# A rotary-embedding kernel: first slab whole, two rows of slab 5 loaded early, slab 7 loaded by GpSimd

**Chip, cores, metric.** One Trainium2 chip, one of its cores. The metric is the device time of one execution in microseconds (us). The span in a profile is 1.8 us shorter than the time (160.4 against 162.2).

## The reference

`x` is 16 x 512 x 1024 float32. Each row of 1024 is 16 heads of 64, and each head is rotated by tables that depend on the position:

```python
x1, x2 = x[..., :half_dim], x[..., half_dim:]
rotated = np.concatenate([x1 * cos - x2 * sin,
                          x1 * sin + x2 * cos], axis=-1)
```

33.55 MB are read and 33.55 MB written, with little arithmetic between.

## The kernel before

The input is cut into 8 slabs of 4 MB: 128 partitions, in each 8 rows of 1024 float32 (32 KB, contiguous in HBM). Five slabs have a place on the chip. ScalarE casts a slab to bfloat16, VectorE does three instructions on it, ScalarE casts it back into the slab's own place, and the store goes out from there. SyncE issues the loads, ScalarE the stores. Load 5 needs the place of slab 0, so it waits until store 0 has landed; load 6 waits for store 1, load 7 for store 2.

```python
nb = 2; slots = 5
nslabs = batch // nb              # 8
rpp = nb * seq // P               # 8 rows per partition
W = rpp * dim                     # 8192 elements = 32 KB

def load(s):
    slab[s] = slabs.tile([P, W], f32, tag="slab", name="slab")
    return nc.sync.dma_start(out=slab[s], in_=dram(x, s))

load(0)
# ... tables cos, sin by nc.gpsimd.dma_start; then load(1) .. load(4) ...

def cast(u):
    s, r, n = u
    if r == 0:
        xb[s] = xpool.tile([P, W], bf16, tag="xb", name="xb")
    nc.scalar.copy(out=view(xb[s], r * dim, (1, n * dim)),
                   in_=view(slab[s], r * dim, (1, n * dim)))

passes = []                       # (slab, first row, rows)
for s in range(nslabs):
    n = rpp if 1 <= s < nslabs - 2 else rpp // 2
    passes += [(s, r, n) for r in range(0, rpp, n)]

cast(passes[0])
for i, (s, r, n) in enumerate(passes):
    if i + 1 < len(passes):
        cast(passes[i + 1])       # the cast of the next pass stands first
    # ... VectorE: tensor_mul, tensor_mul, tensor_add ...
    nc.scalar.copy(out=xs, in_=xu)
    if r + n == rpp:
        nc.scalar.dma_start(out=dram(out_flat, s), in_=slab[s])
        if s + slots < nslabs:
            load(s + slots)
```

Slabs 0, 6 and 7 go in two half passes each (called 6a, 6b, 7a, 7b below), the others whole.

## Time and profile before

| | before |
|---|---|
| time, median of 6 runs | 162.13 us (162.07 to 162.65) |
| span of the profiled run | 160.4 us |
| bytes moved, mean rate | 67.24 MB, 419 GB/s |
| busy: VectorE, ScalarE | 68%, 71% |
| slab 0 landed, slab 1 landed | 13.3, 23.0 us |
| load 5, load 6, load 7 landed | 85.2, 104.6, 123.9 us |
| store 0 issued, store 7 (the last) issued | 37.1, 145.3 us |

The bytes at the rate of the loads that run alone (16 slabs of 9.72 us, 155.5 us) make up nearly the whole span of 160.4, so the DMA engines are the bound here and neither compute engine, busy 68% and 71%, is. A landing is read from the timeline wherever an engine stood idle for it: the cast of slab 5 starts at 85.22, and its bracket says that the DMA released it. The quoted lines are in the prediction. Two words for what follows: a packet is the unit in which the trace records what a DMA engine moves, and a completion is one of the 16 packets of 4 bytes that the trace has for every transfer besides its rows (128 on each of q1 and q10 for 8 slabs, before).

### The profile page before, as it was taken

To read this page: it belongs to the slowest core of one execution; us is meant where nothing else is said; L and a number is where in the kernel's file an instruction comes from. 1 tells how busy PE (TensorE), PEld (TensorE's weight loads), DVE (VectorE), ACT (ScalarE), POOL (GpSimd) and SP (SyncE) were. 2 spreads that over 40 slices of the span, in tenths; PEclk is the share of its full clock that TensorE was granted. 3 is DMA by queue.
4 is the path that set the end of the run, shared out by engine and by line. 5 is a ranking of instruction groups with operands and counts; after the bars stand their busy time and mean duration, and the time that the engine had idled before them with its cause. 6 is when DMAs were issued, how large, how long until landed. Compare 5 with 4: busy or idle time off the path is not lost.

```text
span 160.4 us, 169 instructions
## 1 busy us (share of the span) xinstructions
PE 1.0 (1%) x8; PEld 0.8 (1%) x8; DVE 108.5 (68%) x34; ACT 113.5 (71%) x23; POOL 3.4 (2%) x12
## 2 busy tenths in 40 slices
PE   0011000000000000000000000000000000000000
PEld 0010000000000000000000000000000000000000
DVE  0003799999989979997996099939749599930000
ACT  3006939998998999899907997099995999462000
POOL 7000000000000000000000000000000000000000
DMA  7999999999999999999999999999999999999995
GB/s 245 425 409 409 474 425 400 466 441 392 384 400 400 507 400 400 466 441 392 441 474 392 433 482 392 425 482 400 400 507 400 400 474 433 392 449 466 392 433 221
DMA packets 2368, 67.24 MB, mean 419 GB/s; under 512 B 288, under 2 KB 288, under 8 KB 320
## 3 DMA queue, kind: packets, MB, share of 16 engines
q1 hardware_dynamic: 1152, 33.55, 49.5%
q10 hardware_dynamic: 1152, 33.55, 48.4%
q0 software_dynamic: 64, 0.13, 0.2%
HBM read 33.69 MB, written 33.55 MB: 419 GB/s over the span
## 4 chain that ended last, share of the span: by engine, by line
DMA 59%; ACT 17%; issue 9%; DVE 4%; SPq 0%; ACTq 0%; POOLq 0%
DMA slab<-in_x_dram 39%; DMA out_dram<-slab 15%; ACT slab L146 11%; ACT xb L119 6%; DMA raw<-in_cos_dram 4%; DVE xb L140 1%; DVE xb L143 1%; DVE slab L140 1%; SPq L62 0%; ACTq L146 0%; POOLq L167 0%
## 5 line engine op out<-in xcount | busy, mean ns | idle before, releaser
L119 ACT CAST xb<-slab 128x4096 bf16<-128x4096 f32 (+1 forms) x11 | 56.6, 5155 | 27.5 <-DMA slab<-in_x_dram 26.2
L146 ACT CAST slab<-xb 128x4096 f32<-128x4096 bf16 (+1 forms) x11 | 56.6, 5153 | 3.5 <-DVE xb L143 3.5
L140 DVE TENSOR_TENSOR slab<-xb,tab 128x4096 bf16<-128x4096 bf16 (+1 forms) x11 | 35.9, 3260 | 19.9 <-ACT xb L119 19.8
L140 DVE TENSOR_TENSOR xb<-xb,tab 128x4096 bf16<-128x4096 bf16 (+1 forms) x11 | 35.9, 3261 | 0.3
L143 DVE TENSOR_TENSOR xb<-xb,slab 128x4096 bf16<-128x4096 bf16 (+1 forms) x11 | 35.9, 3261 | 0.3
L110 DVE CAST tab<-acc 128x1024 bf16<-128x1024 f32 x1 | 1.2, 1225 | 12.5 <-PE acc L104 12.5
L119 ACT ACT_TABLE_LOAD x1 | 1.3, 1283 | 0.7 <-PEq L167 0.7
L104 PE MATMUL acc<-tab,pick 128*128 128x128 bf16 x8 | 1.0, 305 | 11.5 <-POOL tab L98 11.5
L92 POOL TENSOR_SCALAR_AFFINE_SELECT pick<-pick 128x128 bf16<-128x128 bf16 x4 | 1.0, 288 | 0.1
L104 PEld LDWEIGHTS <-pick 128*128 128x128 bf16 x8 | 0.8, 136 | 11.4 <-issue 8.0
L73 POOL DMA_DIRECT2D raw<-in_cos_dram x1 | 0.7, 674 | 0.8 <-POOLq L167 0.8
L89 POOL MEMSET pick<- 128x512 bf16 x1 | 0.5, 543 | 0.0
L98 POOL CAST tab<-raw 128x256 bf16<-128x256 f32 x1 | 0.4, 396 | 6.9 <-DMA raw<-in_sin_dram 6.9
L73 POOL DMA_DIRECT2D raw<-in_sin_dram x1 | 0.5, 534 | 0.0
L167 POOL MEMSET const-float32-0.0<- 128x1 f32 x1 | 0.1, 99 | 0.2 <-issue 0.2
L167 POOL MEMSET const-bfloat16-1.0<- 128x1 bf16 x1 | 0.1, 102 | 0.0
L167 POOL MEMSET const-uint8-127<- 128x1 uint8 x1 | 0.1, 102 | 0.0
L167 POOL MEMSET const-float32-1.0<- 128x1 f32 x1 | 0.1, 99 | 0.0
## 6 DMA issues: line engine op xcount, KB each, us to landing
slab<-in_x_dram SPq DMA_DIRECT2D x8, 4096.0 KB, 24.5
out_dram<-slab ACTq DMA_DIRECT2D x8, 4096.0 KB, 26.6
raw<-in_cos_dram POOLq DMA_DIRECT2D x1, 64.0 KB, 7.0
raw<-in_sin_dram POOLq DMA_DIRECT2D x1, 64.0 KB, 9.0
```

What stands on the lines that cost most here:

```text
L73: table[i] = nc.gpsimd.dma_start(out=view(raw, i * TR * half, (1, TR * half)), in_=bass.AP(tensor=src.tensor, offset=src.offset, ap=[[TR * ...
L89: nc.gpsimd.memset(pick, 0.0)
L92: nc.gpsimd.affine_select(out=part, in_=part, compare_op=mybir.AluOpType.not_equal, fill=1.0 if g < G else -1.0, base=-(g % G), pattern=[[ ...
L98: nc.gpsimd.tensor_copy(out=tab1, in_=raw)
L104: nc.tensor.matmul(view(acc, (i * rpp + g * TR) * hd + h * half, (hd, TR), (1, half)), view(pick, (i * h * G + g) * P, (1, P)), view(tab1, ...
L110: nc.vector.tensor_copy(out=tab, in_=acc)
L119: nc.scalar.copy(out=view(xb[s], r * dim, (1, n * dim)), in_=view(slab[s], r * dim, (1, n * dim)))
L140: nc.vector.tensor_mul(out=t, in0=xu, in1=view(tab, a + r * hd, (hd, n), (0, nh), (1, hd)))
L143: nc.vector.tensor_add(out=xu, in0=xu, in1=view(t2, half, (hd, n * nh), (-half, 2), (1, half)))
L146: nc.scalar.copy(out=xs, in_=xu)
L167: nc = _bacc.Bacc("TRN2", target_bir_lowering=False, num_devices=1)
```

## The change

Its intent, as far as the code tells: let slab 0 go through in fewer instructions; have 1 MB of slab 5 on the chip before any place is free, in a buffer of its own; and give load 7 a queue where it need not stand behind load 6.

```diff
+    E = 2 * dim
+    ahead = singles.tile([P, E], f32, tag="ahead")
     def load(s):
+        queue = nc.sync if s < nslabs - 1 else nc.gpsimd
+        a = E if s == slots else 0
         slab[s] = slabs.tile([P, W], f32, tag="slab", name="slab")
-        return nc.sync.dma_start(out=slab[s], in_=dram(x, s))
+        return queue.dma_start(out=view(slab[s], a, (1, W - a)),
+                               in_=dram(x, s, a, W - a))
@@ after the loads 1 to 4
+    nc.sync.dma_start(out=ahead, in_=dram(x, slots, 0, E))
@@ cast
-        nc.scalar.copy(out=view(xb[s], r * dim, (1, n * dim)),
-                       in_=view(slab[s], r * dim, (1, n * dim)))
+        a = E if s == slots else 0
+        nc.scalar.copy(out=view(xb[s], r * dim + a, (1, n * dim - a)),
+                       in_=view(slab[s], r * dim + a, (1, n * dim - a)))
+        if a:
+            nc.scalar.copy(out=view(xb[s], 0, (1, a)), in_=ahead)
@@ passes
-        n = rpp if 1 <= s < nslabs - 2 else rpp // 2
+        n = rpp if s < nslabs - 2 else rpp // 2
```

## The prediction

> **What bounds the kernel now.** I read first the slices and queues of the page, then the chain that ended last, then the timeline.
>
> ```profile
> DMA  7999999999999999999999999999999999999995
> ...
> DMA packets 2368, 67.24 MB, mean 419 GB/s; under 512 B 288, under 2 KB 288, under 8 KB 320
> ...
> q1 hardware_dynamic: 1152, 33.55, 49.5%
> q10 hardware_dynamic: 1152, 33.55, 48.4%
> ```
>
> The DMA engines are full in every slice but the first and the last. Each queue has 1152 packets for 8 transfers, 144 each: 128 rows of 32 KB and 16 completions. So on each of 16 engines a slab is 8 packets of one row and one completion.
>
> ```profile
> 13.33 7.11 ACT L119 CAST xb<-slab 128x4096 bf16<-128x4096 f32 x2 [11.31 <-DMA slab<-in_x_dram]
> ...
> 23.05 7.02 ACT L119 CAST xb<-slab 128x8192 bf16<-128x8192 f32 x1 [2.61 <-DMA slab<-in_x_dram]
> ...
> 85.22 7.02 ACT L119 CAST xb<-slab 128x8192 bf16<-128x8192 f32 x1 [5.05 <-DMA slab<-in_x_dram]
> ...
> 145.28 0.34 ACTq L148 DMA_DIRECT2D out_dram<-slab  x1
> ```
>
> Slab 0 lands at 13.33 and slab 1 at 23.05: one slab alone costs 9.72 us, or 1.215 us per row and engine. Fifteen more slabs (7 loads, 8 stores) give 13.3 + 15 x 9.72 = 159.1, against a span of 160.4. Compute has slack: at most 7.02 + 7.01 us of ScalarE per slab against 19.4 us of transfer. The last store is issued at 145.28 but can't start moving before store 6 is through; counted back from the end, 160.4 - 0.9 - 9.7 = 149.8. So the compute tail has about 4 us of slack[...].
>
> ```profile
> 37.11 24.39 DMA out_dram<-slab
> ...
> 61.59 23.61 DMA slab<-in_x_dram
> ...
> 99.00 24.93 DMA slab<-in_x_dram
> ```
>
> This is the chain: store 0 frees slab 0's place, load 5 follows; load 7 follows store 2. Each takes 24 us, not 9.7, since loads and stores take turns on the engines: 2 x 9.72 = 19.4, and 4 to 5 us of queue.
>
> ```profile
> raw<-in_cos_dram POOLq DMA_DIRECT2D x1, 64.0 KB, 7.0
> raw<-in_sin_dram POOLq DMA_DIRECT2D x1, 64.0 KB, 9.0
> ```
>
> These two lines matter most for the change. A table has 4 KB per engine, 0.15 us of work. Issued at 1.24 and 1.91, they land at 8.25 and 10.9, 2.7 us apart: two turns (4 KB of data, then a completion), each behind a 32 KB row of load 0 (2 x 1.215, and the small ones). **The engines take turns by packets, not by bytes**; a small packet pays for a whole turn.
>
> [...]
>
> **The change, part by part.**
>
> *Whole first slab.* Two half passes become one. VectorE keeps its time (6 x 2.29 = 13.7 against 3 x 4.43 = 13.3). Store 0 comes later: 13.33 + 7.02 + 13.3 + 7.01 = 40.7 instead of 37.1. Loads fill the 3.6 us, since five are queued. Alone it costs nothing: the bytes are the same and the DMA never idles.
>
> *Two rows of slab 5 early.* It moves 1 MB, so no bytes are saved. The cast becomes two, of 6144 and 2048 elements: by the size, 5.3 + 1.9 us for 7.0, so 0.2 us more. But "ahead" is 128 rows of 8 KB: 8 packets of 8 KB per engine and one completion, so 9 turns. It sits behind load 4 on SyncE's queue, when stores are already running:
> - Load 3 ends at 32.8 + 9.7 = 42.5. Store 0 starts moving at about 44.5 (3.8 us after its issue). Load 4 has had 2 us alone; its other 7.7 us take 15.4 us: done at 60. Store 0 is done at 62 and lands at about 63.
> - Ahead: 9 turns beside a 1.215 us store row, and 8 x 0.30 us of its own: 13.3 us where bytes alone ask for 2.4. It ends at 73.5. Store 1 gets 8 rows in that time and lands at about 76.
> - The rest of slab 5 (24 KB rows) waits behind ahead though its place was free at 63. Eight turns of 0.91 + 1.215 and one completion: 17 to 18 us, landing at 91 (before 85.2). Store 2 runs beside it and lands at about 93 (before about 99).
>
> So the early rows make slab 5 late and the stores early, and the stores drain ahead of the compute.
>
> *Load 7 on GpSimd's queue.* On SyncE's queue it waited behind load 6. Now it is issued when store 2 lands, at 93, while load 6 has only begun (at 91). From about 96 three queues take turns. Load 6 has about 6 of 8 rows left: 6 x 3 x 1.215 = 21.9, so it lands at about 118 (before 104.6). Load 7 lands at 122 to 123, no better than 123.9 before.
>
> *What that does to the end.* ScalarE works in order: the first cast of slab 6 stands before the last cast of slab 5, and so before store 5. From load 6 at 117.6:
> - cast 6a 3.6, cast-out of slab 5 7.0, issue and cast 6b 4.0: 132.2
> - VectorE on 6b, 7a and 7b, 6.95 each with small waits on casts 7a and 7b: 154.0
> - cast-out of 7b 3.6: store 7 issued at 157.6 (before 145.3)
> - store 7 alone: 9.7 and 2.7 of issue and landing: 170.3; span about 171.
>
> The DMA would idle about 10 us after store 5. The time is 1.8 above the span (162.2 against 160.4), so this sum gives 172.8.
>
> **The rivals.**
> *A: nothing happens (span 160 to 161).* Needed: turns go by bytes for 8 KB rows, or several rows of a SyncE transfer share a packet, so that ahead takes about 5 us. Then load 5 lands at 85, load 6 at 105, load 7 at 123, and the DMA stays full to the end: 162.2. For it: the DMA line of nines, equal bytes, and that the order of transfers is worth nothing while both queues have work; also that someone wrote these parts to fit a tuned kernel. Against it: the two table loads. But those were GpSimd's, with 512 B rows in one 4 KB packet; how 8 KB rows from SyncE are packed, nothing here shows.
> *B: ahead does hurt, but less.* Delays of a few us in GpSimd's issue let load 6 finish sooner; phases of a turn count for 1 us each. Load 6 at 110 to 114 gives a span of 164 to 168, time 166 to 170. If load 7 then is the last to matter (after it 3.6 + 6.95 x 2 + 3.6 + waits = 21.4, as between 123.9 and 145.3 before), a landing after 126.5 costs us for us.
> *C: worse.* If GpSimd's rows are cut into 4 KB packets, load 7 gets a ninth of each round, lands near 140 and ends the kernel: 140 + 21.4 + 12.4 + 0.9 = 175 span.
> *D: faster.* [...] Over 2% can't come out of this unless the start changes, which no part touches.
>
> **Range and chances.** The main sum (172.8) with B around it has about 0.6, A about 0.35. Lags I can't fix by a few us move the main sum mostly down, so I say 169.5, range 161.5 to 174.5, which holds A as well. Faster 0.03, same 0.36, slower 0.61.
>
> **What would show each step.** Ahead: its issue to landing, or the gap from the landing of slab 4 (cast 4 is not its witness, ScalarE is busy) to the cast of slab 5; the cast of 6144 should start near 91, not 85, released by the DMA. Turns: the rows of ahead under 16 KB in the packet line, and store 1 landing near 76. Load 7: GpSimd's issue at about 93, the cast of slab 6 released near 118. End: DMA slices below 9 after slice 33, last store issued near 157. If the cast of slab 5 comes at 85 and the DMA line stays at 9 up to the end, the step "a small row pays a whole turn" is wrong, and the time will be 162. If load 6 lands before 108 although ahead was slow, the three-way sharing is wrong.

## More of the kernel before

In the trace before, the record of load 1's landing (23.03) follows the end of its last completion (22.58) by 0.45 us. The views of the profile don't list single packets and landings; where the text speaks of the trace's records, they were read from the stored trace.

## The result, and the profile after

Six runs of the changed kernel took 165.89, 166.53, 169.28, 170.25, 171.76 and 171.97 us: median 169.76, against 162.13 before. By the rule that a run over 1.5% above the fastest of its kernel counts as slow, the first two are fast and the other four slow; the clock was 1.0 in all. The ratio of the fast runs is 1.0246 (95% interval 1.0212 to 1.028): slower. Ratios here are the mean time of one kernel's fast runs over that of the other's of the same rounds, so not quite the ratio of the medians. The kernel before stayed within 0.6 us in these rounds, so the spread belongs to the changed kernel; run e8 below looks at it.

The profile is of the fastest run (span 164.1). First its slices and queues, from the page:

```profile
DMA  7999999899989999999999998998989989891885
...
q10 hardware_dynamic: 1152, 33.55, 47.4%
q1 hardware_dynamic: 1152, 29.36, 42.4%
q0 software_dynamic: 208, 4.33, 6.1%
```

The DMA line is nearly full (8 or 9) from slice 2 to slice 36 of 40; the 1 after it is 4 us in which hardly anything moved. SyncE's queue (q1) moves 4 MB less but has as many packets as before: the early rows came as 128 packets of 8 KB and 16 completions. Here a row is a packet, of 8, 24 or 32 KB.

Two lines of the table by stretches, before and after (stretch and its length; busy time of PE, weight loads, VectorE, ScalarE and GpSimd; clock, DMA share, GB/s). Before:

```profile
124.00:157.50 33.50, 0.00 (x0) 0.00 (x0) 15.35 (x7) 17.79 (x5) 0.00 (x0) 1.00 0.99 427
```

After:

```profile
124.00:157.50 33.50, 0.00 (x0) 0.00 (x0) 20.63 (x9) 24.50 (x7) 0.00 (x0) 1.00 0.87 376
```

Here the time goes: in the last stretch the compute engines have more left to do and the DMA waits for them. The timeline after tells why:

```profile
89.02 5.31 ACT L129 CAST xb<-slab 128x6144 bf16<-128x6144 f32 x1 [5.11 <-DMA slab<-in_x_dram]
...
94.40 0.56 POOL L69 DMA_DIRECT2D slab<-in_x_dram  x1 [83.02 <-ACT xb L129]
...
113.23 3.60 ACT L129 CAST xb<-slab 128x4096 bf16<-128x4096 f32 x1 [10.18 <-DMA slab<-in_x_dram]
...
152.13 0.34 ACTq L159 DMA_DIRECT2D out_dram<-slab  x1
```

(The bracket of load 7's issue names a cast, but the issue follows the landing of store 2, at 93.85, by 0.55 us, as it does within 0.01 us in e1, e3, e4, e6, e8 and e12 below, so store 2 is what it waited for.) Slab 5 comes at 89.0 (before 85.2), load 7 is issued at 94.4 (before 99.0), slab 6 comes at 113.2 (before 104.6), and the last store is issued at 152.1 (before 145.3). And the issues with their time to landing:

```profile
slab<-in_x_dram POOLq DMA_DIRECT2D x1, 4096.0 KB, 28.5
slab<-in_x_dram SPq DMA_DIRECT2D x1, 3072.0 KB, 26.0
ahead<-in_x_dram SPq DMA_DIRECT2D x1, 1024.0 KB, 62.0
```

The early rows, issued at 10.05, land at 72.05. Load 4, just ahead of them in the queue, lands at 59.9 by the trace's record of landings; so 1 MB took 12.1 us. The rest of slab 5, issued at 63.0, spends 26 us on 3 MB. In the chain of waits the end now hangs on load 6:

```profile
55.24 21.01 DMA out_dram<-slab
...
76.30 36.90 DMA slab<-in_x_dram
...
113.23 3.60 ACT xb L129
116.83 6.92 ACT slab L157
...
148.50 3.60 ACT slab L157
```

Store 1 lands at 76.25, load 6 follows and takes 36.9 us (the chain before held load 7 there, with 24.9 us), and after it there is compute to the end.

### The profile page after: what moved, and what is told of

It reads as the page before. It is cut to its first block, busy times and chain, and to the rows that moved or that the text cites. A ratio compares the mean times of both kernels' runs of the same rounds, so it can differ in the third digit from the quotient of the medians.

```text
span 164.1 us, 166 instructions
## 1 busy us (share of the span) xinstructions
PE 1.0 (1%) x8; PEld 0.8 (1%) x8; DVE 108.3 (66%) x31; ACT 113.5 (69%) x22; POOL 3.9 (2%) x13
## 3 DMA queue, kind: packets, MB, share of 16 engines
q10 hardware_dynamic: 1152, 33.55, 47.4%
q1 hardware_dynamic: 1152, 29.36, 42.4%
q0 software_dynamic: 208, 4.33, 6.1%
## 4 chain that ended last, share of the span: by engine, by line
DMA 43%; ACT 35%; DVE 12%; issue 2%; ACTq 0%; SPq 0%
DMA slab<-in_x_dram 30%; ACT slab L157 19%; ACT xb L129 15%; DMA out_dram<-slab 13%; DVE xb L151 4%; DVE xb L154 4%; DVE slab L151 4%; ACTq L159 0%; ACTq L157 0%; SPq L69 0%
## 5 line engine op out<-in xcount | busy, mean ns | idle before, releaser
L129 ACT CAST xb<-slab 128x8192 bf16<-128x8192 f32 (+2 forms) x10 | 54.8, 5481 | 30.5 <-DMA slab<-in_x_dram 29.3
L157 ACT CAST slab<-xb 128x8192 f32<-128x8192 bf16 (+1 forms) x10 | 56.5, 5650 | 7.4 <-DVE xb L154 7.3
L151 DVE TENSOR_TENSOR slab<-xb,tab 128x8192 bf16<-128x8192 bf16 (+1 forms) x10 | 35.7, 3571 | 27.0 <-ACT xb L129 21.1
L154 DVE TENSOR_TENSOR xb<-xb,slab 128x8192 bf16<-128x8192 bf16 (+1 forms) x10 | 35.7, 3572 | 0.3
L151 DVE TENSOR_TENSOR xb<-xb,tab 128x8192 bf16<-128x8192 bf16 (+1 forms) x10 | 35.7, 3572 | 0.3
L69 POOL DMA_DIRECT2D slab<-in_x_dram x1 | 0.6, 557 | 83.0 <-ACT xb L129 83.0
L132 ACT CAST xb<-ahead 128x2048 bf16<-128x2048 f32 x1 | 1.9, 1892 | 0.0
```

The source lines that it names most:

```text
L69: return queue.dma_start(out=view(slab[s], a, (1, W - a)), in_=dram(x, s, a, W - a))
L129: nc.scalar.copy(out=view(xb[s], r * dim + a, (1, n * dim - a)), in_=view(slab[s], r * dim + a, (1, n * dim - a)))
L132: nc.scalar.copy(out=view(xb[s], 0, (1, a)), in_=ahead)
L151: nc.vector.tensor_mul(out=t, in0=xu, in1=view(tab, a + r * hd, (hd, n), (0, nh), (1, hd)))
L154: nc.vector.tensor_add(out=xu, in0=xu, in1=view(t2, half, (hd, n * nh), (-half, 2), (1, half)))
```

## The experiments

Theory: the DMA engines take turns by packets. The traces of the kernel before and of the change show turns of this size, by their records of packets, as the median step from one row of a transfer to the next: 1.21 us for load 1 alone, 2.42 for load 5 beside stores (before), 3.63 for the last rows of load 6, with a store and load 7 beside it (the change). An 8 KB early row took 0.31 us itself, and while they moved, the rows of store 1 came mostly 1.51 us apart, where 1.21 and 0.31 make 1.52. The theory goes on: the early rows, small packets placed where stores are in flight, hold up slab 5, while the stores run ahead; load 7 on a third queue then takes turns from load 6; the compute that follows load 6 sets the end. Rivals: (1) GpSimd's queue costs by itself; (2) the whole first slab costs, by its later store 0; (3) the small rows or the split cast cost by themselves, not their turns. Every kernel gave the reference's result. Times are medians of four runs unless noted; landings and issues are from one profiled run of each (in e1, e4 and e5 the slowest of the four).

| run | whole slab 0 | early rows | load 7 on | us | load 6, load 7 land | last store issued |
|---|---|---|---|---|---|---|
| before | no | no | SyncE | 162.1 | 104.6, 123.9 | 145.3 |
| e9 | yes | no | SyncE | 162.6 | 106.0, 125.3 | 146.7 |
| e12 | no | no | GpSimd | 162.4 | 104.1, 123.4 | 144.8 |
| e1 | yes | no | GpSimd | 162.8 | 107.8, 124.7 | 146.7 |
| e11 | no | behind load 4 | SyncE | 166.4 | 111.1, 130.4 | 151.8 |
| e2 | yes | behind load 4 | SyncE | 162.9, slow runs 166.7 | 108.2, 127.6 | 148.9 |
| e3 | no | behind load 4 | GpSimd | 175.9 | 123.2, 124.5 | 162.1 |
| the change | yes | behind load 4 | GpSimd | 165.9 to 172.0 | 113.2, 122.9 | 152.1 |
| e8, a slow run | yes | behind load 4 | GpSimd | 170.6 | 117.9, 125.1 | 156.8 |
| e4 | yes | before load 2 | GpSimd | 164.7 | 112.0, 126.6 | 151.0 |
| e7 | yes | before load 2 | SyncE | 165.1 | 108.6, 127.9 | 149.3 |
| e10 | no | before load 2 | SyncE | 163.0 | 106.8, 126.3 | 147.6 |

The first eight rows are all combinations of the three parts.

**e1: without the early rows**

```diff
-    ahead = singles.tile([P, E], f32, tag="ahead")
-    nc.sync.dma_start(out=ahead, in_=dram(x, slots, 0, E))
-        a = E if s == slots else 0        # in load and cast
+        a = 0
-        if a:                             # in cast
-            nc.scalar.copy(out=view(xb[s], 0, (1, a)), in_=ahead)
```

> The change without the early rows: first slab whole and load 7 on GpSimd's queue remain. Theory (a small row pays a whole turn, so the early transfer delays slab 5): without it slab 5 is cast near 85, load 6 lands near 105, the DMA stays full to the end, 162 to 163 us. Rival 1 (GpSimd's queue is what costs): load 7 still comes on the third queue, so the time stays at 165 to 170. Rival 2 (the whole first slab, store 0 3.7 us later): also 165 or more.

Measured: 162.81 us (161.79 to 163.60), ratio 1.003 (0.9987 to 1.0074), the same. Slab 5 is cast at 87.2. Load 6 lands at 107.8, later than the 105 expected, but the last store is out in time:

```profile
107.79 3.60 ACT L127 CAST xb<-slab 128x4096 bf16<-128x4096 f32 x1 [6.62 <-DMA slab<-in_x_dram]
...
146.69 0.34 ACTq L155 DMA_DIRECT2D out_dram<-slab  x1
```

Without the early rows the loss is gone, though both other parts stay. Rivals 1 and 2 fall as sole causes.

**e2: load 7 back on SyncE's queue**

```diff
-        queue = nc.sync if s < nslabs - 1 else nc.gpsimd
+        queue = nc.sync
```

> The change with load 7 back on SyncE's queue. Theory: the early transfer still lands near 72 to 74 and slab 5 near 89; load 6 no longer shares with load 7, so it lands near 109 rather than 113, but load 7 waits behind it and lands near 128 to 130; last store issued near 150, span 163 to 165, time 164.5 to 167: about what the change has, with another cause at the end. Rival 1 (GpSimd's queue costs): back to 162.2.

Measured: 162.92, 162.94, 166.66 and 166.81 us. Load 6 lands at 108.2, five us sooner than in the change; load 7 now stands behind it and decides:

```profile
127.62 3.60 ACT L129 CAST xb<-slab 128x4096 bf16<-128x4096 f32 x1 [1.83 <-DMA slab<-in_x_dram]
...
148.94 0.34 ACTq L159 DMA_DIRECT2D out_dram<-slab  x1
```

The first cast of slab 7 starts as load 7 lands. The landings are a little under the expectation. The time expected was 164.5 to 167; the slow runs meet it, the fast ones do not and are close to before. Fast runs against fast runs, the change takes 3.3 us more than e2 (166.2 on average against 162.9), so GpSimd's queue does add to the loss, but only with the early rows behind load 4: e12 below has none, and with the early rows before load 2 it makes no difference to the time (e4 and e7: 164.7 with it, 165.1 without).

**e3: slab 0 in halves again**

```diff
-        n = rpp if s < nslabs - 2 else rpp // 2
+        n = rpp if 1 <= s < nslabs - 2 else rpp // 2
```

> The change with slab 0 in two halves as before; early rows and GpSimd's queue remain. Theory: store 0 is 3.6 us earlier, so more of the load queue, the early transfer's turns included, runs beside stores: early transfer lands near 74 to 76, slab 5 near 91 to 93, load 6 near 117 to 121, time 170 to 176, slower than the change. Rival 2 (the whole first slab costs): back toward 162.

Measured: 175.93 us (175.85 to 176.03), ratio 1.0843 (1.0827 to 1.0859): ten us worse than the change's fast runs, a time within the expectation. The early rows land at 77.2, slab 5 at 94.2, load 6 at 123.2, 1.2, 1.2 and 2.2 us after the ranges expected:

```profile
91.32 0.56 POOL L69 DMA_DIRECT2D slab<-in_x_dram  x1 [79.84 <-DMA out_dram<-slab]
...
123.20 3.60 ACT L129 CAST xb<-slab 128x4096 bf16<-128x4096 f32 x1 [14.96 <-DMA slab<-in_x_dram]
...
162.11 0.34 ACTq L159 DMA_DIRECT2D out_dram<-slab  x1
```

Load 7 is issued at 91.3, before load 6 moves its first row (93.1 by the trace's records of packets). Load 7's own first row moves at 95.8, when load 6 has begun little over one of its eight rows on each engine, so nearly all of load 6 goes in three-way turns: from its first row to its landing it takes 30.1 us, where 8 x 3 x 1.215 are 29.2. The whole first slab is the part that softens the change: it holds the stores back by 3.7 us (store 0 is issued at 40.85 in the change, at 37.19 here).

**e4: the early rows issued between load 1 and load 2**

```diff
     for s in range(1, slots):
+        if s == 2:
+            nc.sync.dma_start(out=ahead, in_=dram(x, slots, 0, E))
         tc.add_manual_dep(load(s).ins, ...)
-    nc.sync.dma_start(out=ahead, in_=dram(x, slots, 0, E))
```

> The change with one thing moved: the early transfer is issued between load 1 and load 2, when no store is in flight; same bytes, same 8 KB rows, same packets. Theory (turns beside stores): it lands about 2.5 us after slab 1, near 25.5, slab 5 near 84 to 86, load 6 near 104 to 106, DMA full to the end, 162 to 163 us. Rival 3 (8 KB and 24 KB rows are slow in themselves, or the split cast costs): still 165 to 170. Rival 1 (third queue): still above 164.

Measured: 164.71 us (164.42 to 165.52), ratio 1.0159 (1.0127 to 1.0191), clear of 1. The transfer itself did as expected; its time to landing fell from 62.0 to 16.9 us and it ended at 25.4, 2.5 us after slab 1 (22.9):

```profile
ahead<-in_x_dram SPq DMA_DIRECT2D x1, 1024.0 KB, 16.9
```

So the same 8 KB rows cost 2.5 us where no store is in flight and 12.1 us beside stores. That is the theory's central step, shown. But the kernel did not come back to 162: slab 5 was cast at 88.4 and load 6 landed at 112.0. The expectation missed (162 to 163), and by the time alone rival 1 (above 164) would stand; e7 and e10 pursue it.

**e5: the early rows as two transfers of one row each**

```diff
-    nc.sync.dma_start(out=ahead, in_=dram(x, slots, 0, E))
+    for h in range(2):
+        nc.sync.dma_start(out=view(ahead, h * dim, (1, dim)),
+                          in_=dram(x, slots, h * dim, dim))
```

> The change with its early transfer as two transfers of one 4 KB row per partition: same bytes, 18 turns per engine instead of 9. Theory (turns): the second lands near 83 to 85 instead of 72, slab 5 near 99 to 102 instead of 89, load 6 near 120 to 123; the last store is issued 38.9 us after load 6 lands, so near 160, and the time is 172 to 178. If turns went by bytes, doubling the packets would change nothing: 166 to 172 as the change itself.

Measured: 179.64 us (178.43 to 180.69), ratio 1.108 (1.1027 to 1.1133).

```profile
96.84 5.31 ACT L130 CAST xb<-slab 128x6144 bf16<-128x6144 f32 x1 [12.87 <-DMA slab<-in_x_dram]
...
127.75 3.60 ACT L130 CAST xb<-slab 128x4096 bf16<-128x4096 f32 x1 [16.88 <-DMA slab<-in_x_dram]
```

By the record of landings the two ended at 70.7 and 79.2, so 19.4 us after load 4 (59.8) for the same bytes; slab 5 was cast at 96.8 and load 6 landed at 127.7. More turns, more delay: the direction is the theory's, the sizes are off both ways (less delay for the rows than the 83 to 85 said, more for load 6, which here had begun only 0.8 rows per engine when load 7 joined at 95.8; the time, too, is above the 172 to 178 expected).

**e6: one early row instead of two**

```diff
-    E = 2 * dim
+    E = dim
```

> The change with one early row per partition instead of two: half the early bytes, 4 KB rows, the same 9 turns; the rest of slab 5 has 28 KB rows. Theory (turns): the early transfer lands only 1 to 1.5 us sooner, near 71, slab 5 near 89 as in the change, load 6 near 113, time 165 to 172 as the change. If the cost went by the bytes taken out of turn, half of it would go: slab 5 near 87, time 163 to 165.

Measured: 165.78, 166.18, 170.58 and 171.73 us; ratio of the fast runs 1.024 (1.022 to 1.026), the change's own.

```profile
ahead<-in_x_dram SPq DMA_DIRECT2D x1, 512.0 KB, 60.9
```

The early row lands at 71.15, 10.9 us after load 4, though it carries half the bytes; load 6 lands at 113.5. **Half the bytes, the same turns, the same loss**: here the cost went by turns (10.9 us for 0.5 MB, 12.1 for 1 MB).

**e7: early rows before load 2, load 7 on SyncE's queue**

```diff
 (as e4, and)
-        queue = nc.sync if s < nslabs - 1 else nc.gpsimd
+        queue = nc.sync
```

> The early transfer before load 2 as in the run before, and load 7 back on SyncE's queue. In that run slab 5 was cast at 88.4 and load 6 landed at 112.0, which my theory had not foreseen; its rest was laid to load 6 and load 7 taking turns. If so, load 6 now lands at 106 to 109, load 7 near 126 to 128, the last store is issued near 148 to 149, and the time is 162 to 163. If load 6 still lands at 111 or later, something in the early rows themselves (24 KB rows, engines out of step) holds it back, and the time stays near 164.5.

Measured: 165.06 us (164.69 to 165.42), ratio 1.019 (1.0173 to 1.0207), called unclear against the 2% line. Load 6 at 108.6, load 7 at 127.9 and the last store at 149.3 are about as expected, so most of load 6's delay in e4 (112.0) was due to the third queue. The time is not: with the last store at 149.3 it should have been 163. Here another loss shows, of the DMA itself. Of e7 the stretch from 60 to 100 us:

```profile
60.00:100.00 40.00, 0.00 (x0) 0.00 (x0) 33.58 (x9) 36.03 (x7) 0.00 (x0) 1.00 1.01 416
```

and of the kernel before:

```profile
60.00:100.00 40.00, 0.00 (x0) 0.00 (x0) 33.17 (x8) 33.70 (x5) 0.00 (x0) 1.00 1.00 433
```

Over 40 us 17 GB/s less are 0.7 MB, or 1.6 us at 433 GB/s, with the engines as busy (share 1.01 against 1.00): rows took longer. By the trace's records of packets a 32 KB row of a load took 1.34 us on average in this stretch, against 1.21 before. e4 has 411 GB/s in the same stretch.

**e8: the change once more, for a profile**

> The change itself once more for a profile, because its six runs lie between 165.9 and 172.0 and only one profile (164.1 span) is at hand. Theory: the time follows load 6. If the span is 168 or more, load 6 lands at 117 or later and the last store is issued 38.9 us after it. If instead a slow profile shows load 6 near 113 and the end late for another reason (slower DMA turns, load 7 after 130, a stretched ScalarE), the theory does not explain the spread.

Measured: 170.56 us, span 168.8. At 2.8% above the change's fastest run it belongs with the slow ones. From its chain and its timeline:

```profile
76.52 41.32 DMA slab<-in_x_dram
```

```profile
117.87 3.60 ACT L129 CAST xb<-slab 128x4096 bf16<-128x4096 f32 x1 [12.51 <-DMA slab<-in_x_dram]
...
156.78 0.34 ACTq L159 DMA_DIRECT2D out_dram<-slab  x1
```

Load 6 takes 41.3 us instead of 36.9, lands 4.7 us later, and the last store is issued 38.9 us after it, as in the fast run; the span is 4.7 us longer. So this slow run is the same mechanism with a larger size. The trace's record of landings says where: of load 6's 16 completions 14 come at 112.8 to 113.1, as all 16 do in the fast run (112.9 to 113.2), and two come at 117.8; the cast of slab 6 starts at 117.87, after those two. Two completions of load 4 were already late (60.9 and 61.0, the others by 59.8), and two of the rest of slab 5 (90.8 and 91.3, the others by 88.9). So it seems that two engines of 16 fell a row (1.2 us) behind before the early rows moved; the landings don't name the engines, and what put them behind is open. The same split into two levels shows in e2 (162.9 and 166.7) and e6 (166.0 and 171.2 on average), which have the whole first slab and early rows behind load 4 too, and not so wide in e5, which has both as well (2.3 us), nor in e3 and e11, which lack the whole slab (0.2 and 1.2 us): an observation, not a test.

**e9: only the whole first slab**

> The kernel before with only the first slab whole. Theory: store 0 is issued at 40.8 instead of 37.1, the DMA stays full, load 6 lands near 105, last store issued near 146, time 162 to 162.6. Rival 2: if the late store 0 itself costs, as the profile of the run without early rows (span 161.8) would allow, 163 to 164.

```diff
 (the kernel before, and)
-        n = rpp if 1 <= s < nslabs - 2 else rpp // 2
+        n = rpp if s < nslabs - 2 else rpp // 2
```

Measured: 162.59 us, ratio 1.0013 (0.9982 to 1.0044). Store 0 is issued at 41.0 and nothing follows from it. Rival 2 falls.

**e10: only the early rows, before load 2**

> The kernel before with only the early rows, issued before load 2; slab 0 in halves, load 7 on SyncE's queue. In the run with the whole first slab the time stayed at 165.1 though the last store was issued at 149.3; between 60 and 100 us the DMA moved 416 GB/s in place of the 432 of before. If the early rows and the 24 KB rows of slab 5 cause that (rows and engines out of step), this one also stays at 164 to 165.5 with 410 to 420 GB/s in that stretch. If the later store 0 of the whole first slab is needed for it, this one comes back to 162 to 163 with 430 GB/s.

```diff
 (the kernel before with ahead and the split cast, and)
     for s in range(1, slots):
+        if s == 2:
+            nc.sync.dma_start(out=ahead, in_=dram(x, slots, 0, E))
```

Measured: 163.03 us (162.21 to 163.08), ratio 1.0032 (1.0002 to 1.0062).

```profile
60.00:100.00 40.00, 0.00 (x0) 0.00 (x0) 31.84 (x8) 33.29 (x6) 0.00 (x0) 1.00 1.00 432
```

The rate is back at 432. So 8 KB rows, 24 KB rows and the split cast cost next to nothing by themselves: rival 3 falls. The low rates of e4 and e7 (411 and 416) came only with the early rows before load 2 together with the whole first slab. But e1, without early rows, has a little of it too (430 GB/s, 1.26 us for a load's row), and e5 more (425), each in one profile, so what makes the rows slow stays open.

**e11: only the early rows, where the change has them**

> The kernel before with only the early rows, in the place the change gives them (behind load 4), load 7 on SyncE's queue. Theory: as in the run without GpSimd's queue but with store 0 3.6 us earlier: the early rows land at 74 to 77, slab 5 at 91 to 94, load 6 at 110 to 114, load 7 behind it at 129 to 133. Then load 7 decides: last store 21.3 us after it, at 150 to 154, span 12 us later, time 164 to 168. Rival (GpSimd's queue is needed for the loss): 162 to 163, as with the same rows issued before load 2 (163.0).

```diff
 (the kernel before with ahead and the split cast, and after the loads 1 to 4)
+    nc.sync.dma_start(out=ahead, in_=dram(x, slots, 0, E))
```

Measured: 166.40 us (165.77 to 166.93), ratio 1.0253 (1.0215 to 1.0291). The same transfer before load 2 (e10) gave 163.0: its place in the queue is worth 3.4 us.

```profile
ahead<-in_x_dram SPq DMA_DIRECT2D x1, 1024.0 KB, 67.0
```

While its 128 rows of 8 KB moved, the stores moved 116 rows of 32 KB by the trace's records of packets: nearly one for one. The early rows land at 77.1, slab 5 at 94.1, and load 7 decides:

```profile
94.10 5.31 ACT L129 CAST xb<-slab 128x6144 bf16<-128x6144 f32 x1 [13.90 <-DMA slab<-in_x_dram]
...
130.47 3.60 ACT L129 CAST xb<-slab 128x4096 bf16<-128x4096 f32 x1 [1.82 <-DMA slab<-in_x_dram]
...
151.79 0.34 ACTq L159 DMA_DIRECT2D out_dram<-slab  x1
```

**e12: only GpSimd's queue**

> The kernel before with only load 7 on GpSimd's queue. Theory: load 7 is issued at 99 when store 2 lands, load 6 has by then most of its rows, and the three queues meet only for a few turns: load 6 lands at 104 to 107, load 7 at 124 to 126, last store at 145 to 147.5, time 162 to 163. Rival: the third queue costs by itself: 164 or more.

```diff
 (the kernel before, and)
+        queue = nc.sync if s < nslabs - 1 else nc.gpsimd
-        return nc.sync.dma_start(out=slab[s], in_=dram(x, s))
+        return queue.dma_start(out=slab[s], in_=dram(x, s))
```

Measured: 162.41 us (162.39 to 162.46), ratio 1.0009 (0.9992 to 1.0025). Rival 1 falls as a cost by itself. This run also shows GpSimd's issue of load 7 beside a running VectorE instruction:

```profile
96.24 4.42 DVE L147 TENSOR_TENSOR xb<-xb,tab 128x8192 bf16<-128x8192 bf16 x1
...
99.72 0.56 POOL L68 DMA_DIRECT2D slab<-in_x_dram  x1 [88.24 <-DMA out_dram<-slab]
```

The issue takes 0.56 us beside a running VectorE instruction, just as in the change, where VectorE was idle.

No version here beats the kernel before, and the best that the parts do is to leave its time as it was.

## Why the prediction was right

- **Direction and mechanism held.** The early rows delayed slab 5, the stores ran ahead, load 7 took turns from load 6, the compute after load 6 set the end. e11 against e10 (166.4 against 163.0) shows the first link by the place alone, e5 and e6 that it went by turns, e12 and e3 that the third queue hurt only with the early rows behind load 4 (162.4 alone; e11 to e3, 166.4 to 175.9).
- **The intermediate times held to about 2 us.** Early rows at 72.1 (73.5 said), store 1 at 76.3 (76), slab 5 at 89.0 (91), load 7 issued at 94.4 (93), load 7 landed at 122.9 (122 to 123). For the rest of slab 5 the prediction's own terms add up to 18.2 us, where it wrote 17 to 18; 16.9 were measured.
- **Load 6 was over-sized**: 113.2 where 117.6 went into the sum. I had the third queue start at about 96; load 7's first row moved at 100.4, 6 us after its issue. So two-way turns lasted longer: by the trace's records of packets load 6, from its first row at 89.5, had begun five of its eight rows on each engine by then, where the prediction left six to go. The last three began at 101.6, 105.2 and 108.9, each 3.6 us = 3 x 1.215 after the one before, and the completions landed by 113.2. The three-way turns were right, their start was not.
- **The tail was over-sized by 2.5 us.** From load 6 to the last store I had 40.0; the change, e1, e3, e4 and e8 all show 38.9. From the last store's issue to the end I had 13.4 (the terms written add up to 13.3: 170.0 and not 170.3 for the landing); it was 12.0, for issue and landing, 2.7 in the sum (my estimate; before, load 0 took 12.6 from issue to landing, 2.9 above the 9.7 of a slab), took 1.2 with the engines idle: the first row moved 0.85 us after the issue. With the 4.4 of load 6 that is the 6.9 us between the sum (span 171) and the fast profile (164.1). The idle time of the DMA engines was over-sized with it: I had 10 us after store 5; by the records they idle from 149.2 to 153.0, after store 6.
- **A second rule was in rival B and showed in e2, e7 and e11**: if load 7 is the late one, the last store follows it by 21.3 us (127.6 to 148.9, 130.4 to 151.8). The last store is issued at the later of load 6 + 38.9 and load 7 + 21.3.
- **The point of 169.5 lies 3.3 us above the fast runs (166.2 on average) and at the lower end of the slow ones (169.3 to 172.0).** That it stands near the median of all six (169.76) is luck: I did not foresee that one kernel would spread over 6 us. By the fast runs the loss was put too high (7.3 us said, 4.0 measured). The range of 161.5 to 174.5 held "nothing happens" too, so that the time fell into it shows little; the landings show more.
- **Rival A (nothing happens) fell** on the point it rested on: packets of SyncE's early transfer are one row each, as the 1152 packets on its queue show, and it took 12.1 us where A needed about 5.
- **Rivals C and D did not come**: GpSimd's 128 rows moved as 32 KB packets (4.33 MB in 208 packets, tables and completions included), and nothing was faster.

## What to carry to other kernels

In these runs, where several DMA queues were busy, their packets moved in turn (the last rows of load 6 began 3.63 us apart with three queues at work in the change, rows of a load alone 1.21), and rows of 4 to 32 KB were a packet each (the tables' rows of 512 B went eight to a packet). So a transfer with 8 KB rows beside stores with 32 KB rows got about one row for one (128 against 116 in e11, 128 against 112 in the change), took 12.1 us in the change where it took 2.5 in e4 with no store in flight, and held up slab 5 behind it in its queue (landed at 89.0, before at 85.2). In a kernel like this one, put short-row transfers where no other queue is busy (e10: 163.0, e11: 166.4), or leave them out (e1: 162.8). From issue to first row it took 6.0 us for load 7 (the change), 3.9 for load 7 (e4) and 3.8 for store 0 (before) with the engines full, and 0.85 for the last store with the engines idle (the change). And in this kernel, bound by bytes, moving a load earlier or giving it a queue of its own gained nothing (e10: 163.0, e12: 162.4, before: 162.1), and together, with the early rows behind load 4, they starved the load that the next compute needed (e3: load 6 landed at 123.2, before at 104.6); look at which landing the last store hangs on, and how far behind it comes.
